# First block's end: order of logits and weight low parts, of pooling and short convolution, of the output units' parts, and layer norm's PSUM banks

## The chip, the cores and the metric

One core of a Trainium2 chip runs the whole program. The metric is the device time of one execution in microseconds (us), as the median of several runs.

## The reference

Two blocks run one after the other on 512 tokens of width 1024. The change concerns the first block alone:

```python
h = rms_norm(x, norm1_g); z = h @ w_in                    # 1024 -> 9 x 256
y_pool  = pool_mixer(z_pool, pool_w, pool_scale)          # running means over 2, 4, 8, 16 tokens, then 64x64 matrices
y_sconv = s_b * causal_dwconv(s_c * s_h, sconv_w)         # 3 taps
u = c_a * sigmoid(c_g); u = causal_dwconv(u, conf_dw_w) + conf_dw_b     # 31 taps
y_conf  = silu(layer_norm(u, conf_ln_g, conf_ln_b))
y_attn  = diff_attention(q, k, v, ...)                    # 4 heads, two softmaxes each, bias by distance
x = x + concat([y_pool, y_sconv, y_conf, y_attn]) @ w_out
x = x + (silu(h2 @ w_gate) * (h2 @ w_up)) @ w_down        # h2 = rms_norm(x, norm2_g)
```

The second block prepends 16 meta tokens and has two layers of its own.

## The kernel before, in words

Activations lie with features on the partitions and tokens along the row. Every large product is made of three matmuls of 128x128 by 128x512 in a reduced-precision float format: a value is split into a high part (a cast, ScalarE) and a low part (value minus high part, VectorE), and high x high, high x low and low x high are summed in PSUM. `f_acc` (L171, matmuls at L179) does this for one output tile of 128 features: 8 input tiles give 24 matmuls. After each group of three it calls `tick`, which emits the next piece of a background generator, here attention.

Weights come by `weights` (L145): SP loads 512 KB into one of two buffers `wraw`, ScalarE casts it in two halves to `whi` (L164), VectorE makes the two low parts `wlo` (L165), each with four buffers, so that two sets of weights are present. A load waits until the low parts of the set two before it are made; a cast waits until TensorE has used the tile it overwrites.

The order on each engine is set by a scheduler at build time. It takes instructions by priority as their inputs become ready in its own model of time. `first()` gives a raised priority (weights, evacuations), `chain()` a far higher one (offset 100000), and `behind(ins, name)` an order edge between two instructions of one engine. On the chip each engine then works its list strictly in order.

`layer1` (L493) is the first block's mixer. In order of the program: the gates of the long convolution (ca, cg), values, keys and queries; attention starts as a background pipeline (`pipe` with the stages `logits`, `wait`, `turn`, `values`, `wait`, `finish`, 16 items, one step per three ticks). `logits` makes two score tiles in the PSUM banks "a" (L656), reduces each on VectorE with the bias added (L658), exponentiates on ScalarE (L660), and combines the two softmaxes (L665 to L667). `turn` transposes them in banks "b" (L209), `values` multiplies by v (L686). The long convolution of 31 taps is 60 instructions on VectorE (L725) with ordinary priority, so they fill its gaps; its result is y. Then four projections by `fproj` (two output tiles each): z for pooling, two for the short convolution (sc, evacuated by L740), and sb (evacuated by L552). After these stand the pooling chain (L745 to L759), the short convolution (L760 to L766), `mix` of its two rows, the pool matrices (L770, L772) and `mix` of their two rows. `mix` splits a result into a high part (cast, L117) and a low part (L118) in one of the four `mx` buffers, which the gates and the short convolution's temporaries use in turn as well. Then layer norm of y: sums over features by matmul (L779, L787, L248) in the PSUM banks "b", the last product at L798.

The output projection is made in two halves by `add_out` (L332): first pooling and short convolution (`mixed[:4]`, L799), then attention and conformer rows (`mixed[4:]`), each in four units of two output tiles; each tile takes its four rows in order, 12 matmuls, and is added to x (L356). `add_out` has an argument `late=n` that makes the first unit take the first n rows for both its tiles before the others; these calls don't use it. `finish(att)` between the halves emits what is left of attention.

At the start, `setup` (L375) loads x in tiles and the first two sets of weights by the queues of SP and ScalarE in an order written by hand. `layer1` splits x (L257 and L258) and these weights (L511 and L512), and the first 48 matmuls (L579) follow tile by tile. `tables` (L458) builds the tables of the position bias on GpSimd: it loads relb and the meta tokens by GpSimd's own DMA queue (L469, L470), copies runs of buckets (L482), writes the tables to DRAM (L484) and later reads the bias tile B from there (L490).

Of the kernel before, what the change touches and what calls it, by code (L numbers as in the profile page):

```python
# [18 lines left out]
S = 512  # L19
# [46 lines left out]
class Kern:  # L66
# [78 lines left out]
    def weights(self, nk, ncol):  # L145

        if self.ahead:
            return self.ahead.pop(0)
        src = self.io["w"]
        n = nk * ncol  # L150
        out = [], []
        with self.first():
            raw = self.wp.tile([128, 1024], F32, name="wraw", bufs=2)
            self.queue(self.nc.sync, raw[:, :n], bass.AP(tensor=src.tensor, offset=src.offset + self.wi, ap=[[n, 128], [1, n]]))
            step = 512 // ncol
            for k0 in range(0, nk, step):
                k1 = min(k0 + step, nk)
                c = slice(k0 * ncol, k1 * ncol)
                w = c.stop - c.start
                if self.keep:  # L160
                    hi, lo = (self.row(n) for n in ("hhi", "hlo"))
                else:
                    hi, lo = (self.wp.tile([128, 512], F32R, name=n, bufs=4) for n in ("whi", "wlo"))
                self.nc.scalar.copy(hi[:, :w], raw[:, c])  # L164
                self.lo.tensor_tensor(out=lo[:, :w], in0=raw[:, c], in1=hi[:, :w].bitcast(F32), op=OP.subtract)  # L165
                for t, o in zip((hi, lo), out):
                    o += [t[:, k * ncol:(k + 1) * ncol] for k in range(k1 - k0)]
            self.wi += 128 * n
        return out
# [205 lines left out]
    def setup(self):  # L375
# [9 lines left out]
        with self.first():  # L385
# [13 lines left out]
            w(nc.scalar, 1, 0, 512)  # L399
            w(nc.sync, 0, 256, 512)  # L400
            x(nc.scalar, 1, 2)
# [56 lines left out]
    def tables(self):  # L458
# [4 lines left out]
        with self.tc.tile_pool(name="setup", bufs=1) as p:  # L463

            rb = p.tile([128, 3, 32], F32, name="relb")
            for h in range(4):
                src = self.io["relb"]
                src = bass.AP(tensor=src.tensor, offset=src.offset + 32 * h, ap=[[0, COPIES], [128, 3], [1, 32]])
                nc.gpsimd.dma_start(rb[h * COPIES:(h + 1) * COPIES], src)  # L469
            nc.gpsimd.dma_start(self.xs[:, :, 0:M], io["meta"].rearrange("k p t -> p k t"))  # L470
# [22 lines left out]
    def layer1(self):  # L493
# [44 lines left out]
        with tc.tile_pool(name="l1", bufs=1, reuse_waits="tile") as p:  # L538
# [4 lines left out]
            def fproj(out, evac=None):  # L543
                for f in range(2):
                    w = self.weights(8, 128)
                    ps = self.mm()
# [100 lines left out]
            def logits(i, h):  # L647
# [5 lines left out]
                for m in range(2):  # L653
# [3 lines left out]
                    with self.chain():  # L657
                        nc.vector.tensor_tensor_reduce(out=e, in0=ps[:, :W], in1=B1[:, h, 384 - 128 * i:],  # L658
                                                       scale=-1.0, scalar=BIG, op0=OP.add, op1=OP.min, accum_out=st[:, m:m + 1])
# [4 lines left out]
                with self.chain():  # L664
                    nc.vector.reciprocal(r, st[:, 2:4])  # L665
                    nc.vector.tensor_scalar(r[:, 1:2], r[:, 1:2], st[:, 2:3], lam[:, 0:1], op0=OP.mult, op1=OP.mult)
# [74 lines left out]
            fproj(sb)  # L741
            mixed = [None] * 8
            with self.chain():
# [16 lines left out]
                nc.vector.tensor_tensor(out=sc[:, :, PADS:], in0=sc[:, :, PADS:], in1=rb2[:, None, :].to_broadcast([128, 2, S]), op=OP.mult)  # L760
                sw = self.cols[:, COLS["sconv"][0]:COLS["sconv"][0] + 6].rearrange("p (f k) -> p f k", f=2)
                for f in range(2):
                    nc.scalar.mul(sh[:, f], sc[:, f, 0:S], sw[:, f, 0:1])
                    for k in (1, 2):
                        nc.vector.scalar_tensor_tensor(sh[:, f], sc[:, f, k:k + S], sw[:, f, k:k + 1], sh[:, f], op0=OP.mult, op1=OP.add)
                    nc.vector.tensor_tensor(out=sb[:, f], in0=sb[:, f], in1=sh[:, f], op=OP.mult)  # L766
                    mixed[2 + f] = self.mix(sb[:, f], M, T)
# [6 lines left out]

            ones = self.m1
            with self.chain():
                ps = self.ch("b")
# [6 lines left out]
                ps = self.ch("b")  # L784
# [5 lines left out]
                ps = self.ch("b")  # L790
# [8 lines left out]
            self.add_out(mixed[:4], X)  # L799
# [11 lines left out]
            self.add_out(mixed[4:], X, after)  # L811
# [999 lines left out]
```

## Time and profile before

| | |
|---|---|
| median of 3 runs | 1182.95 us (1182.59 to 1184.75) |
| profiled execution | 1182.28 us |
| its span | 1180.5 us |
| TensorE busy | 1157.7 us, 98% |
| VectorE busy | 792.2 us, 67% |
| ScalarE busy | 627.4 us, 53% |
| GpSimd busy | 66.9 us, 6% |
| instructions | 18912 |

The span runs from the first to the last instruction of the profile; the run's time holds a little more around it. TensorE's share is high over the whole span, so the rows below look at stretches of it: the first 30 us and the first block's end, from 100 to 180 us. A bracket behind an instruction gives the idle time of its engine before it, and what ended it. An instruction counts as busy from its modelled start to its end; matmuls overlap, so that a record may be longer than the pace at which they follow each other.

### The profile page before, as it was taken

What the parts mean: (1) busy time and instruction counts of PE and PEld (TensorE: products, weight loads), DVE (VectorE), ACT (ScalarE), POOL (GpSimd) and SP (SyncE); (2) the same over time, 40 slices, a digit from 0 to 9 for tenths busy, and PEclk for the clock granted to TensorE, in tenths of its full rate; (3) what the DMA queues carried; (4) which work ended last, traced back from release to release, by engine and by line L of the source; (5) the groups of instructions that cost most, each with busy time, mean ns of one, the idle gap of its engine ahead of it and who ended that gap; (6) DMA issues with size and microseconds to landing.
All of it is one profiled execution on the core that took longest, in us unless ns stands there. A gap on an engine that the chain in (4) does not pass through costs nothing.

```text
span 1180.5 us, 18912 instructions
## 1 busy us (share of the span) xinstructions
PE 1157.7 (98%) x7094; PEld 994.4 (84%) x7094; DVE 792.2 (67%) x1765; ACT 627.4 (53%) x1404; POOL 66.9 (6%) x175
## 2 busy tenths in 40 slices
PE   8999799999999999999999999999999999999997
PEld 6988588888888888888899899899999888887786
DVE  7999957544433444445799999666567476776782
ACT  6578646433322333344546346667555488777533
POOL 8000002000000000002000000000011000000000
PEclk9999999999999999999999999999999999999999
DMA  7421112332233233223322112222223221421221
GB/s 245 123 83 54 52 56 90 98 99 91 84 99 114 97 95 102 78 95 126 104 72 72 55 54 72 74 72 75 71 66 127 79 72 55 108 61 53 85 72 72
DMA packets 32908, 101.83 MB, mean 86 GB/s; under 512 B 4128, under 2 KB 4960, under 8 KB 32816
## 3 DMA queue, kind: packets, MB, share of 16 engines
q1 hardware_dynamic: 30784, 96.48, 26.3%
q0 software_dynamic: 880, 2.25, 0.7%
q10 hardware_dynamic: 1152, 1.89, 0.5%
q8 instruction: 56, 0.92, 0.3%
q14 instruction: 36, 0.29, 0.1%
HBM read 96.42 MB, written 3.10 MB: 84 GB/s over the span
## 4 chain that ended last, share of the span: by engine, by line
PE 87%; DVE 8%; ACT 2%; DMA 1%; issue 1%; POOL 0%; DVEq 0%; ACTq 0%; POOLq 0%; SPq 0%
PE mm L179 70%; PE psb L209 3%; DVE wlo L165 2%; DVE y L725 2%; PE pso L1187 1%; PE pso L1443 1%; PE psa L1580 1%; PE mm L1580 1%; PE psa L1428 1%; DVE sc L1041 1%; PE pso L686 1%; PE psb L1428 1%; DVE m L1040 1%; DMA x<-in_x 1%; PE psa L1149 1%
## 5 line engine op out<-in xcount | busy, mean ns | idle before, releaser
L179 PE MATMUL mm<-hhi,whi 128*128 128x512 f32 (+2 forms) x1280 | 432.4, 338 | 0.0
L179 PE MATMUL mm<-hhi,wlo 128*128 128x512 f32 (+2 forms) x1280 | 426.0, 333 | 2.9 <-DVE wlo L165 2.9
L179 PE MATMUL mm<-hlo,whi 128*128 128x512 f32 (+2 forms) x1280 | 425.1, 332 | 0.0
L164 ACT CAST whi<-wraw 128x512 fp32r<-128x512 f32 x346 | 205.2, 594 | 277.9 <-PE mm L179 251.4
L165 DVE TENSOR_TENSOR wlo<-wraw,whi 128x512 fp32r<-128x512 f32 x346 | 231.1, 671 | 137.6 <-ACT whi L164 118.0
L179 PEld LDWEIGHTS mm<-hhi,wlo 128*128 128x128 f32 x1280 | 241.5, 189 | 25.3 <-DVE wlo L165 3.0
L179 PEld LDWEIGHTS mm<-hhi,whi 128*128 128x128 f32 x1280 | 241.9, 189 | 23.0 <-issue 1.4
L179 PEld LDWEIGHTS mm<-hlo,whi 128*128 128x128 f32 x1280 | 241.5, 189 | 20.9 <-issue 0.2
L179 PE MATMUL mm<-mx,whi 128*128 128x512 f32 (+2 forms) x384 | 92.5, 333 | 5.8 <-ACT mx L117 5.6
L179 PEld LDWEIGHTS mm<-mx,whi 128*128 128x128 f32 x384 | 64.8, 192 | 12.9 <-ACT mx L117 6.3
L830 DVE TENSOR_TENSOR gu<-mm,rb 128x512 f32<-128x512 f32 x44 | 30.4, 691 | 66.8 <-PE mm L179 66.8
L271 POOL TENSOR_TENSOR acc<-acc,sq 128x528 f32<-128x528 f32 (+1 forms) x18 | 25.6, 1423 | 771.8 <-ACT sq L269 771.8
L179 PE MATMUL mm<-hidh,whi 128*128 128x512 f32 x176 | 68.5, 389 | 0.0
L179 PE MATMUL mm<-hidh,wlo 128*128 128x512 f32 x176 | 68.5, 389 | 0.0
L179 PE MATMUL mm<-hidl,whi 128*128 128x512 f32 x176 | 68.5, 389 | 0.0
L179 PE MATMUL mm<-mx,wlo 128*128 128x512 f32 (+2 forms) x192 | 61.9, 324 | 0.0
L725 DVE SCALAR_TENSOR_TENSOR y<-u,cols,y 128x512 f32<-128x512 f32 x60 | 42.3, 742 | 0.1
L370 DVE TENSOR_TENSOR tmp<-mm,rb 128x272 f32<-128x272 f32 (+2 forms) x60 | 28.8, 479 | 17.6 <-PE mm L179 17.0
L356 DVE TENSOR_TENSOR x<-x,mm 128x512 f32<-128x512 f32 (+2 forms) x56 | 29.8, 535 | 15.0 <-PE mm L179 14.7
L179 PEld LDWEIGHTS mm<-mx,wlo 128*128 128x128 f32 x192 | 36.6, 191 | 2.7 <-issue 0.2
L179 PEld LDWEIGHTS mm<-hidh,whi 128*128 128x128 f32 x176 | 33.0, 188 | 6.9
L179 PEld LDWEIGHTS mm<-hidl,whi 128*128 128x128 f32 x176 | 33.0, 188 | 6.8
(444 smaller groups left out, 1820.9 us busy)
## 6 DMA issues: line engine op xcount, KB each, us to landing
wraw<-in_w SPq DMA_DIRECT2D x144, 512.0 KB, 3.5
wraw<-in_w SPq DMA_DIRECT2D x16, 384.0 KB, 3.0
wraw<-in_w SPq DMA_DIRECT2D x16, 320.0 KB, 2.8
bh<-tab SPq DMA_DIRECT2D x16, 132.0 KB, 3.6
mx<-cqk SPq DMA_DIRECT2D x8, 132.0 KB, 4.9
x<-in_x SPq DMA_DIRECT2D x4, 256.0 KB, 5.0
B<-tab POOLq DMA_DIRECT2D x4, 256.0 KB, 8.7
out<-L ACTq DMA_DIRECT2D x4, 256.0 KB, 2.4
```

The costliest lines, as they stand in the source:

```text
L164: self.nc.scalar.copy(hi[:, :w], raw[:, c])
L165: self.lo.tensor_tensor(out=lo[:, :w], in0=raw[:, c], in1=hi[:, :w].bitcast(F32), op=OP.subtract)
L179: nc.tensor.matmul(ps[b], lhsT=ww[i][:, f0:f0 + nf], rhs=aa[:, t0:t1], start=first and i == 0 and j == 0, stop=last and i == n - 1 and j == 2)
L209: self.nc.tensor.transpose(out, in_, self.ident[:n, :n])
L271: e.tensor_tensor(out=acc[:, c0:c1], in0=acc[:, c0:c1], in1=sq[:, c0:c1], op=OP.add)
L356: nc.vector.tensor_tensor(out=x, in0=x, in1=p, op=OP.add)
L370: self.nc.vector.tensor_tensor(out=out[:, t0:t1], in0=p, in1=rb[:nf, t0:t1], op=OP.mult)
L686: nc.tensor.matmul(o[:, h * 64:h * 64 + 64], lhsT=pT[:, j * 128:(j + 1) * 128], rhs=vt[:, j, h * 64:h * 64 + 64], start=j == 0, stop=j == i)
L725: nc.vector.scalar_tensor_tensor(y[:, f], u[:, f, k:k + S], cw[:, f, k:k + 1], y[:, f], op0=OP.mult, op1=OP.add)
L830: nc.vector.tensor_tensor(out=t[:, g], in0=ps, in1=rbx, op=OP.mult)
L1428: nc.tensor.matmul(z, lhsT=self.trir[:n, :n], rhs=part, start=False, stop=True, skip_group_check=True)
L1580: nc.tensor.matmul(ps[half], lhsT=aa[:, k], rhs=ww[:, :512], start=False, stop=k == 3 and j == 2, skip_group_check=True)
```

## The change

It has six parts.

1. `weights` remembers the name of the last low part that it issued (`self.last`), and each logits reduction (L658) gets an order edge behind it.
2. The projection sb moves behind pooling and the pool matrices. Its evacuation is now `short`, which multiplies by the norm's factor and, for the first tile, does the whole short convolution; each tile's `mix` follows. With `then=(4, 256)` the first set of the output projection's weights is loaded before the second tile's matmuls.
3. Layer norm's three PSUM tiles come from the banks "a" (of the logits), not "b".
4. Both halves of the output projection take `late=2`: their first unit takes the first two rows (pooling, attention) for both tiles first.
5. The small step at L666 is a scalar_tensor_tensor instead of a tensor_scalar.
6. At the start, the second set's first weight load is halved with the second x tile between the halves, and relb and the meta tokens are loaded by SP's queue instead of GpSimd's.

```diff
--- before.py
+++ after.py
@@ -162,7 +162,7 @@
                 self.nc.scalar.copy(hi[:, :w], raw[:, c])
-                self.lo.tensor_tensor(out=lo[:, :w], in0=raw[:, c], in1=hi[:, :w].bitcast(F32), op=OP.subtract)
+                self.last = self.lo.tensor_tensor(out=lo[:, :w], in0=raw[:, c], in1=hi[:, :w].bitcast(F32), op=OP.subtract).ins.name
                 for t, o in zip((hi, lo), out):
@@ -396,9 +396,10 @@
             w(nc.sync, 0, 0, 256)
-            w(nc.scalar, 1, 0, 512)
+            w(nc.scalar, 1, 0, 256)
+            x(nc.scalar, 1, 2)
             w(nc.sync, 0, 256, 512)
-            x(nc.scalar, 1, 2)
+            w(nc.scalar, 1, 256, 512)
             x(nc.sync, 2, 3)
@@ -466,8 +467,8 @@
                 src = bass.AP(tensor=src.tensor, offset=src.offset + 32 * h, ap=[[0, COPIES], [128, 3], [1, 32]])
-                nc.gpsimd.dma_start(rb[h * COPIES:(h + 1) * COPIES], src)
-            nc.gpsimd.dma_start(self.xs[:, :, 0:M], io["meta"].rearrange("k p t -> p k t"))
+                nc.sync.dma_start(rb[h * COPIES:(h + 1) * COPIES], src)
+            nc.sync.dma_start(self.xs[:, :, 0:M], io["meta"].rearrange("k p t -> p k t"))
@@ -540,9 +541,11 @@
-            def fproj(out, evac=None):
+            def fproj(out, evac=None, then=None):
                 for f in range(2):
                     w = self.weights(8, 128)
+                    if f == 1 and then:
+                        self.ahead.append(self.weights(*then))
                     ps = self.mm()
@@ -655,15 +658,17 @@
                     with self.chain():
-                        nc.vector.tensor_tensor_reduce(out=e, in0=ps[:, :W], in1=B1[:, h, 384 - 128 * i:],
-                                                       scale=-1.0, scalar=BIG, op0=OP.add, op1=OP.min, accum_out=st[:, m:m + 1])
+                        ins = nc.vector.tensor_tensor_reduce(out=e, in0=ps[:, :W], in1=B1[:, h, 384 - 128 * i:],
+                                                             scale=-1.0, scalar=BIG, op0=OP.add, op1=OP.min, accum_out=st[:, m:m + 1])
...
+                        self.behind(ins.ins, self.last)
                         nc.scalar.activation(e, e, AF.Exp, scale=-1.0, bias=st[:, m:m + 1], accum_out=st[:, 2 + m:3 + m])
...
                     nc.vector.reciprocal(r, st[:, 2:4])
-                    nc.vector.tensor_scalar(r[:, 1:2], r[:, 1:2], st[:, 2:3], lam[:, 0:1], op0=OP.mult, op1=OP.mult)
+                    nc.vector.scalar_tensor_tensor(r[:, 1:2], r[:, 1:2], st[:, 2:3], lam[:, 0:1], op0=OP.mult, op1=OP.mult)
                     nc.vector.scalar_tensor_tensor(es[0], es[1], r[:, 1:2], es[0], op0=OP.mult, op1=OP.add)
@@ -738,7 +743,6 @@
             fproj(None, evac=lambda f, ps: nc.vector.tensor_tensor(out=sc[:, f, PADS:], in0=ps, in1=sc[:, f, PADS:], op=OP.mult))
-            fproj(sb)
             mixed = [None] * 8
@@ -757,14 +761,6 @@
                     nc.vector.tensor_tensor(out=z[:, f, PADP:], in0=a[:, PADP:], in1=z[:, f, PADP:], op=OP.subtract)
-                nc.vector.tensor_tensor(out=sc[:, :, PADS:], in0=sc[:, :, PADS:], in1=rb2[:, None, :].to_broadcast([128, 2, S]), op=OP.mult)
-                sw = self.cols[:, COLS["sconv"][0]:COLS["sconv"][0] + 6].rearrange("p (f k) -> p f k", f=2)
-                for f in range(2):
-                    nc.scalar.mul(sh[:, f], sc[:, f, 0:S], sw[:, f, 0:1])
-                    for k in (1, 2):
-                        nc.vector.scalar_tensor_tensor(sh[:, f], sc[:, f, k:k + S], sw[:, f, k:k + 1], sh[:, f], op0=OP.mult, op1=OP.add)
-                    nc.vector.tensor_tensor(out=sb[:, f], in0=sb[:, f], in1=sh[:, f], op=OP.mult)
-                    mixed[2 + f] = self.mix(sb[:, f], M, T)
             for f in range(2):
@@ -772,22 +768,38 @@
+            def short(f, ps):
...
+                nc.vector.tensor_tensor(out=sb[:, f], in0=ps, in1=rbx, op=OP.mult)
+                with self.chain():
+                    if f == 0:
+                        nc.vector.tensor_tensor(out=sc[:, :, PADS:], in0=sc[:, :, PADS:], in1=rb2[:, None, :].to_broadcast([128, 2, S]), op=OP.mult)
+                        sw = self.cols[:, COLS["sconv"][0]:COLS["sconv"][0] + 6].rearrange("p (f k) -> p f k", f=2)
+                        for i in range(2):
+                            nc.scalar.mul(sh[:, i], sc[:, i, 0:S], sw[:, i, 0:1])
+                            for k in (1, 2):
+                                nc.vector.scalar_tensor_tensor(sh[:, i], sc[:, i, k:k + S], sw[:, i, k:k + 1], sh[:, i], op0=OP.mult, op1=OP.add)
+                    nc.vector.tensor_tensor(out=sb[:, f], in0=sb[:, f], in1=sh[:, f], op=OP.mult)
+                    mixed[2 + f] = self.mix(sb[:, f], M, T)
...
+            fproj(None, evac=short, then=(4, 256))
...
             ones = self.m1
             with self.chain():
-                ps = self.ch("b")
+                ps = self.ch("a")
                 for f in range(2):
...
                     nc.scalar.square(ysq[:, f], y[:, f])
-                ps = self.ch("b")
+                ps = self.ch("a")
                 for t in range(4):
...
                 self.rstd(yr, ps[:, :4], 256, True)
-                ps = self.ch("b")
+                ps = self.ch("a")
                 for t in range(4):
@@ -796,7 +808,7 @@
                     nc.vector.tensor_tensor(out=y[:, f], in0=y[:, f], in1=ysq[:, f], op=OP.mult)
-            self.add_out(mixed[:4], X)
+            self.add_out(mixed[:4], X, late=2)
             self.finish(att)
@@ -808,7 +820,7 @@
-            self.add_out(mixed[4:], X, after)
+            self.add_out(mixed[4:], X, after, late=2)
         return act2, acc
...
     def ffn(self, act, acc):
```

## Rows read from the trace of the kernel before

**Rows 1.** Page, part 1: busy time of TensorE (PE) and of its weight loads (PEld) and the other engines, share of the span, instructions.

```profile
PE 1157.7 (98%) x7094; PEld 994.4 (84%) x7094; DVE 792.2 (67%) x1765; ACT 627.4 (53%) x1404; POOL 66.9 (6%) x175
```

**Rows 2.** Waits of TensorE from 60 to 180 us: who waited, for whom; us in total, times, longest us.

```profile
PE mm L179 <- ACT mx L117: 5.3, 1, 5.3
PE mm L179 <- DVE wlo L165: 2.9, 1, 2.9
```

**Rows 3.** Chain that ended last, in order of time: start us, us, engine, tile and line, number of instructions. The first piece opens the first output unit of the first half of the output projection; the second is the long stretch of the feed-forward part.

```profile
146.82 5.07 PE mm L179 x12
...
204.46 358.84 PE mm L179 x1583
```

**Rows 4.** Windows of TensorE: length, PE busy us (instructions), granted clock as a share of full speed, DMA share, GB/s.

```profile
141.40:146.80 5.40, 0.13 (x1) 0.78 0.41 145
146.80:151.70 4.90, 4.88 (x12) 0.54 0.19 75
```

**Rows 5.** TensorE in order of time: start us, us, line, operation, out<-in, count, and in brackets the idle time before it and what ended it. The first is in the last short-convolution projection, the second the first layer-norm sum over the second half of y.

```profile
138.96 0.50 PE L179 MATMUL mm<-hhi,wlo 128*128 128x512 f32 x1 [2.86 <-DVE wlo L165]
...
151.72 1.02 PE L779 MATMUL psb<-y,m 128*128 128x512 f32 x2
```

**Rows 6.** VectorE (DVE) in order of time, same columns: low parts of weights (L165), evacuations of the short-convolution projection (L552) and their products (L766), low parts of the mixed rows (L118), the long convolution (L725), the last product of the conformer branch (L798).

```profile
113.51 0.69 DVE L165 TENSOR_TENSOR wlo<-wraw,whi 128x512 fp32r<-128x512 f32 x1
...
136.19 0.67 DVE L552 TENSOR_TENSOR sb<-mm,rb 128x512 f32<-128x512 f32 x1
...
138.22 0.68 DVE L165 TENSOR_TENSOR wlo<-wraw,whi 128x512 fp32r<-128x512 f32 x1
...
143.71 0.68 DVE L552 TENSOR_TENSOR sb<-mm,rb 128x512 f32<-128x512 f32 x1
...
144.91 0.69 DVE L766 TENSOR_TENSOR sb<-sb,mx 128x512 f32<-128x512 f32 x1
...
146.89 1.29 DVE L118 TENSOR_TENSOR mx<-z,mx 128x512 fp32r<-128x512 f32 x2
148.09 1.53 DVE L725 SCALAR_TENSOR_TENSOR y<-u,cols,y 128x512 f32<-128x512 f32 x2
...
167.99 0.68 DVE L798 TENSOR_TENSOR y<-y,ysq 128x512 f32<-128x512 f32 x1
```

**Rows 7.** ScalarE (ACT) in order of time, same columns: casts of weights (L164) and of mixed rows (L117).

```profile
115.82 0.62 ACT L164 CAST whi<-wraw 128x512 fp32r<-128x512 f32 x1
...
124.96 0.61 ACT L164 CAST whi<-wraw 128x512 fp32r<-128x512 f32 x1
...
145.63 0.62 ACT L117 CAST mx<-sb 128x512 fp32r<-128x512 f32 x1 [2.04 <-DVE sb L766]
146.15 1.13 ACT L117 CAST mx<-z 128x512 fp32r<-128x512 f32 x2
...
175.62 0.62 ACT L117 CAST mx<-yT 128x512 fp32r<-128x512 f32 x1 [3.09 <-PE mm L179]
...
177.19 1.14 ACT L117 CAST mx<-y 128x512 fp32r<-128x512 f32 x2
```

**Rows 8.** Window of all engines, from 105.3 to 138.2 us: length, busy us (instructions) of PE, PEld, DVE, ACT and POOL, granted clock, DMA share, GB/s.

```profile
105.30:138.20 32.90, 30.81 (x175) 25.55 (x173) 30.40 (x94) 25.28 (x71) 0.00 (x0) 1.00 0.06 20
```

**Rows 9.** Groups of VectorE's instructions in the same window: shapes and count, busy us, mean ns of one, idle us before them and releaser.

```profile
L765 DVE SCALAR_TENSOR_TENSOR mx<-mx,cols 128x512 f32<-128x512 f32 x4 | 3.0, 745 | 0.0
L666 DVE TENSOR_SCALAR rd<-rd,st,rowp 128x1 f32<-128x1 f32 x10 | 2.7, 268 | 0.0
L725 DVE SCALAR_TENSOR_TENSOR y<-u,cols,y 128x512 f32<-128x512 f32 x3 | 2.2, 732 | 0.0
...
L665 DVE RECIPROCAL rd<-st 128x2 f32<-128x2 f32 x10 | 1.6, 158 | 0.5 <-ACT e L660 0.5
...
L760 DVE TENSOR_TENSOR mx<-mx,rb 128x1024 f32<-128x1024 f32 x1 | 1.2, 1216 | 0.0
```

**Rows 10.** GpSimd (POOL) in order of time: the copies that build the first bias table, and the issue of the loads of the bias tile B.

```profile
8.57 5.35 POOL L482 COPY t<-relb 128x399 f32<-128x399 f32 x14 [3.75 <-DMA relb<-in_relb]
...
26.65 2.21 POOL L490 DMA_DIRECT2D B<-tab  x4
```

**Rows 11.** Instructions of line L658, the reduction of a logits tile: count, ns min/median/max, first and last start us, shapes.

```profile
L658 DVE CUSTOM_DVE_ANT_0 e<-psa,B x32: 276/481/693, 86.1 to 133.5; 128x128 f32<-128x128 f32 x8, 128x256 f32<-128x256 f32 x8, 128x384 f32<-128x384 f32 x8, 128x512 f32<-128x512 f32 x8
```

**Rows 12.** Page, part 6: loads of B: count, KB each, median us from issue to landing.

```profile
B<-tab POOLq DMA_DIRECT2D x4, 256.0 KB, 8.7
```

**Rows 13.** Waits of the SP queue (its DMA issues) from 0 to 190 us.

```profile
SPq L140 <- DVE wlo L165: 132.3, 20, 27.7
```

**Rows 14.** The start, all engines in order of time: row 6.09 is the first pair of weight low parts, 7.15 the second x tile's high part, 8.57 the second pair of weight low parts, 10.43 the fourth x tile's high part, 13.07 the low parts of x tiles 5 to 8, 14.52 the first matmul that waited for them.

```profile
6.09 0.76 DVE L512 TENSOR_TENSOR wlo<-mx,whi 128x256 fp32r<-128x256 f32 x2 [0.33 <-ACT whi L511]
...
7.15 0.72 ACT L257 ACTIVATE hhi<-x,cols 128x512 fp32r<-128x512 f32 x1 [0.78 <-DMA x<-in_x]
...
8.57 1.07 DVE L512 TENSOR_TENSOR wlo<-mx,whi 128x256 fp32r<-128x256 f32 x2
...
10.43 0.72 ACT L257 ACTIVATE hhi<-x,cols 128x512 fp32r<-128x512 f32 x1 [1.33 <-DMA x<-in_x]
...
13.07 3.38 DVE L258 SCALAR_TENSOR_TENSOR hlo<-x,cols,hhi 128x512 fp32r<-128x512 f32 x4
...
14.52 0.49 PE L579 MATMUL psa<-hlo,whi 128*128 128x512 f32 x1 [0.86 <-DVE hlo L258]
```

## Prediction

> **What bounds the kernel now.** I read the page first: TensorE is busy 1157.7 us, 98% of the span [rows 1], so all that any change of order can win is the 22.8 us in which it is not, and what it loses at a lower clock. Then the waits of TensorE from 60 to 180 us: only two count, 2.9 us for a low part of weights and 5.3 us for the cast of a mixed row [rows 2]. Both lie at the first block's end. The chain in order of time shows a third loss there: the 12 matmuls behind the second wait take 5.07 us, 0.42 us each, where the 1583 matmuls of the long feed-forward stretch take 358.84 us, 0.227 us each [rows 3]. The granted clock is 0.54 in that stretch, near the lower of its two levels (1.2 GHz; the upper is 2.4), and TensorE had been idle before it [rows 4]. At 0.227 us the 12 would take 2.72 us, so 2.35 us are lost. Together 2.86 + 5.29 + 2.35 = **10.5 us** hang on this one place.
>
> Why it waits: VectorE. From 105.3 to 138.2 us it is busy 30.40 of 32.90 us [rows 8], nearly all of it the attention chain, which has priority over the weights' low parts. The cast at 115.82 gave the high part, its low part came at 138.22; the previous one came at 113.51, so for 24.7 us there was none [rows 6, 7]. TensorE stood for exactly this one at 138.96 [rows 5]. The second wait is a chain: the last projection is evacuated at 143.71, multiplied at 144.91, cast at 145.63 [rows 6, 7]. TensorE's first matmul there takes a pooling row, but that row's cast stands behind on ScalarE, at 146.15, its low part at 146.89 [rows 6, 7].
>
> **The change part by part.** The sum is made against the profiled execution, 1182.28 us (span 1180.5); the median of the runs is 1182.95, 0.67 higher, and I add that at the end.
>
> *Logits behind low parts.* Every logits reduction follows the last weight low part issued before it. This removes the 2.86 us wait. What is queued behind the waiting reduction is the rest of VectorE's attention chain, and TensorE's next logits, which have two PSUM banks. A set's buffers come free two projections earlier (the cast at 115.82 is for the set used from about 126), so ordinarily the low part is ready long before and the edge costs nothing but order. Only the set loaded ahead (`then`) is tight: its cast stands at 124.96, as the projection before ends [rows 7]; then 0.62 us of cast and 0.68 us of low part stand ahead of one logits step. Between 0 and 1.3 us; I take 0.3, since VectorE has other chain work meanwhile.
>
> *Pooling first, short convolution later.* The two pool matmuls (same cost, other place), casts and low parts come before the last projection and their mx buffers are those of the gates, free since long. The output unit starts with 12 pooling matmuls, 12 x 0.227 = 2.72 us, which cover the last evacuation (0.68), product (0.69), cast and low part: 143.71 to the end of the cast at 146.25 is 2.54 us [rows 3, 6, 7]. So the 5.29 us and the slow clock go if VectorE keeps up. It must do in that window, beside what it does now: three low parts (2.0 us) and the two pooling low parts (1.29 us) [rows 6]; the short convolution (1.2 + 3.0 us) [rows 9] changes place but stays. The step L666 becomes a scalar_tensor_tensor: bounded by its old 268 ns (no gain) and by the 158 ns of the small reciprocal [rows 9]; nearest in shape is the latter, so 10 x 0.11 = 1.1 us less. The 2.2 us of long convolution (y) can slip out of it [rows 9]. 30.40 + 2.0 + 1.3 - 1.1 - 2.2 = 30.4 us of work beside 30.81 us on TensorE [rows 8]: even. VectorE's idle 2.5 us of now may return as a wait on TensorE: 0 to 2.5 us, I take 0.8.
>
> *Layer norm in the logits' banks; second half.* The y that slips is done later. Now y ends at 149.62 and the conformer row at 168.67 [rows 6], 19.05 us of chain. VectorE's total work is unchanged, so I leave y's end there. The banks let attention's last transposes go without queueing behind layer norm's sums; its end is then early and no limit. The first half of the output projection runs from 146.82 to about 175.6, when the first attention row can be cast [rows 3, 7]: 28.8 us, less 2.35 of slow clock. If it starts near 139, TensorE is at the second half at 165.4 and, with attention's 12 matmuls first, needs the conformer rows at 168.2, plus their cast and low part from 168.67: about 2 us late. The chain should lose the 2.1 us until its first sum at 151.72 [rows 5, 6], which stood behind slow matmuls. Between 0 and 3.5 us; I take 1.0.
>
> *The start.* The first load of weights on ScalarE's queue is halved and the second x tile goes between; relb and meta leave GpSimd's queue for SP's, five issues. ScalarE waits 0.78 us for the second x tile and 1.33 us for the fourth [rows 14]; the first gets earlier, the fourth has the same bytes ahead of it. TensorE waits 0.86 us at 14.52 for a low part of a group whose four take 3.38 us [rows 14]. Between 1.5 us gained and 0.5 lost (one more issue ahead of later tiles); I take 0.5 gained. On SP the issues fall into its wait for weight buffers and cost nothing. The copies on GpSimd move some 8 us later, and B with them; the cover is wide (second rival).
> As to those copies, the pair of low parts at 8.57, beside them, took 1.07 us where the pair at 6.09 took 0.76 [rows 10, 14]. The Trainium skill (GPSIMD Engine Reference, 1. Specifications) says that GpSimd's way to SBUF is shared with VectorE and contends with instructions that read two SBUF inputs; by that the start would win its full 1.5 us, and the sum would be 1 us lower. I stay with 0.5, since the copies may take from VectorE later what they leave it here.
>
> Sum: 1182.28 - 10.5 + 0.3 + 0.8 + 1.0 - 0.5 = 1173.4; with 0.67 for the median, **1174.0 us**.
>
> **The rivals.**
> *A (forecast), 0.58:* as above, 1171 to 1177.
> *B, 0.22: the conformer branch becomes the bound.* With TensorE 10 us earlier, y is still filler on a full VectorE, and layer norm's sums stand in TensorE's fixed order. If y slips by the 3 us and the chain keeps its 19 us, TensorE waits 5 us for the conformer rows instead of 1: 1178. For it: VectorE 92% busy [rows 8]. Against: it still stood idle for 2.5 us there.
> *C, 0.11: it does not do what it says.* The scheduler keeps y and the short convolution in front of the last evacuation. Low parts come early, but the same VectorE work ends at 148.2 less its 2.5 us of idle time: the second wait and the slow clock stay in large part, and what the first wait gave goes into waiting for logits: about 1181.
> *D, 0.09, slower: the bias table comes too late.* relb's issue is now in SP's queue, which stands 132.3 us in 20 waits for weight low parts [rows 13]. From the copies' start at 8.57 to B's issue at 26.65 and landing 8.7 us later, 28.9 us with the issuing (2.21), to the first logits at 86.1 [rows 10 to 12], there are some 48 us to spare. If relb stood behind enough weight loads to land after 57 us, the logits, and TensorE in its fixed order, wait us for us; at 70 us that is 13 us against 10 gained: 1186. Against: 132 of SP's 190 us are such waits, so that issues which wait for nothing find free places early.
>
> **How the numbers follow.** The time is A's. The range: below, all new waits at nought and the start at 1.5: 1170.9, so 1170.5; above, B and A's bounds, to 1180.0. C and D, 0.20, are left out. A change under 0.2% (2.4 us) can't be told from none. Faster by that: A, B and little of C, 0.82; same: most of C, 0.10; slower: D, 0.08.
>
> **What would show it.** Right: no wait of TensorE over 1 us between 100 and 165 us, the clock at 1.00 throughout, low parts evenly spaced between the logits, the first mixed-row matmul near 139 us, the feed-forward part starting some 9 us earlier. B: a wait for the cast of y or for layer norm, near 165. C: the waits of the before still there at other sizes. D: first logits after 87 us. Wrong at the root, if TensorE has no idle time there and the span has not fallen by it.

## The result, and the profile after

The changed kernel takes 1176.34 us (median of 4 runs, 1175.28 to 1177.78) against 1183.07 before: a ratio of 0.9941, interval 0.9929 to 0.9953, 6.7 us less. The forecast was 1174.0 in a range of 1170.5 to 1180.0. The profiled execution of after is the longest of its four, 1177.78 us (span 1176.0).

Page, part 1, of after, to be set against [rows 1]: busy time, share of the span and instructions of each engine.

```profile
PE 1159.9 (99%) x7094; PEld 996.0 (85%) x7094; DVE 791.5 (67%) x1765; ACT 625.6 (53%) x1404; POOL 57.4 (5%) x170
```

TensorE's idle time has gone from 22.8 to 16.1 us with the same 7094 matmuls, while its busy time is 2.2 us longer, so that the span of this execution is 4.5 us shorter. Where the idle time went is read from TensorE's waits in after, 60 to 180 us, against [rows 2]:

```profile
PE mm L179 <- ACT mx L117: 2.2, 1, 2.2
PE mm L179 <- DVE mx L118: 0.2, 1, 0.2
```

The 2.9 and the 5.3 us are gone; what stands here is another wait, later and for another row. The windows of after show the place (length, busy us and instructions of PE, PEld, DVE, ACT and POOL, granted clock, DMA share, GB/s), against [rows 4, 8]:

```profile
100.00:120.00 20.00, 20.00 (x108) 16.63 (x107) 19.69 (x68) 15.66 (x51) 0.00 (x0) 1.00 0.25 80
120.00:140.00 20.00, 20.00 (x116) 16.58 (x114) 17.74 (x47) 14.32 (x36) 0.00 (x0) 1.00 0.16 53
140.00:160.00 20.00, 20.00 (x101) 15.91 (x100) 17.84 (x37) 8.01 (x20) 0.00 (x0) 1.00 0.24 79
160.00:172.00 12.00, 9.83 (x53) 7.58 (x51) 7.37 (x16) 9.07 (x24) 0.00 (x0) 1.00 0.14 44
172.00:177.00 5.00, 4.83 (x15) 3.75 (x15) 3.60 (x7) 2.57 (x5) 0.00 (x0) 0.66 0.15 35
```

From 100 to 160 us TensorE never stops and the clock stays at 1.00. Then come 2.17 us of wait and, behind it, 15 matmuls in 4.83 us at a mean clock of 0.66; at the 0.227 us of [rows 3] they would take 3.4, so 1.4 us are lost there. The chain of after in order of time (start us, us, what) names the new wait's cause, and answers to [rows 3]:

```profile
163.18 1.70 PE mm L179 x7
164.88 0.47 PE psa L248 x4
165.35 0.23 PE mm L179
165.58 0.23 PE psb L209 x2
165.81 0.02 issue
165.84 0.48 ACT yT L715
166.31 1.41 ACT y L808 x2
167.72 1.04 ACT ysq L218 x2
168.76 1.04 ACT ysq L219 x2
169.80 0.53 ACT ysq L220
170.33 0.02 issue
170.35 1.29 DVE y L810 x2
171.65 0.61 DVE mx L118
172.26 0.04 issue
172.30 27.06 PE mm L179 x111
...
200.57 4.58 PE mm L179 x20
```

The last attention row is ready at 166.3 (yT, L715), but its cast stands on ScalarE behind four us of the conformer branch's activations and starts at 170.74. The feed-forward stretch starts at 200.57 instead of 204.46, 3.9 us earlier.

### The profile page after: what moved, and what is told of

Same layout as the page of the kernel before. It is cut to its first block, busy times and chain, and to the rows that moved or that the text cites. A ratio compares the mean times of both kernels' runs of the same rounds, so it can differ in the third digit from the quotient of the medians.

```text
span 1176.0 us, 18907 instructions
## 1 busy us (share of the span) xinstructions
PE 1159.9 (99%) x7094; PEld 996.0 (85%) x7094; DVE 791.5 (67%) x1765; ACT 625.6 (53%) x1404; POOL 57.4 (5%) x170
## 4 chain that ended last, share of the span: by engine, by line
PE 87%; DVE 8%; ACT 2%; DMA 1%; issue 1%; SPq 0%; POOL 0%; DVEq 0%; ACTq 0%; POOLq 0%
PE mm L179 70%; PE psb L209 3%; DVE y L730 2%; DVE wlo L165 2%; PE pso L1199 1%; PE pso L1455 1%; PE psa L1592 1%; PE mm L1592 1%; PE pso L691 1%; PE psa L1440 1%; DVE sc L1053 1%; DMA wraw<-in_w 1%; PE psb L1440 1%; DVE m L1052 1%; PE psa L1161 1%
## 5 line engine op out<-in xcount | busy, mean ns | idle before, releaser
L164 ACT CAST whi<-wraw 128x512 fp32r<-128x512 f32 x346 | 205.1, 594 | 285.6 <-PE mm L179 262.5
L165 DVE TENSOR_TENSOR wlo<-wraw,whi 128x512 fp32r<-128x512 f32 x346 | 231.1, 671 | 139.9 <-ACT whi L164 119.7
L370 DVE TENSOR_TENSOR tmp<-mm,rb 128x272 f32<-128x272 f32 (+2 forms) x60 | 28.8, 480 | 17.6 <-PE mm L179 17.1
L356 DVE TENSOR_TENSOR x<-x,mm 128x512 f32<-128x512 f32 (+2 forms) x56 | 29.8, 535 | 14.0 <-PE mm L179 13.4
L179 PEld LDWEIGHTS mm<-hidh,wlo 128*128 128x128 f32 x176 | 33.0, 188 | 6.8
```

The costliest lines, as they stand in the source:

```text
L165: self.last = self.lo.tensor_tensor(out=lo[:, :w], in0=raw[:, c], in1=hi[:, :w].bitcast(F32), op=OP.subtract).ins.name
L179: nc.tensor.matmul(ps[b], lhsT=ww[i][:, f0:f0 + nf], rhs=aa[:, t0:t1], start=first and i == 0 and j == 0, stop=last and i == n - 1 and j == 2)
L356: nc.vector.tensor_tensor(out=x, in0=x, in1=p, op=OP.add)
L370: self.nc.vector.tensor_tensor(out=out[:, t0:t1], in0=p, in1=rb[:nf, t0:t1], op=OP.mult)
```

## The experiments

Three parts of the change are looked at apart: the **edge** (logits behind low parts), the **move** (last projection behind the pooling rows, short convolution in its evacuation, with the small parts: the start, the set split ahead, pairs of rows first, L671) and the **banks** (layer norm's PSUM tiles). With before and after, the twelve runs cover all eight combinations. The kernel before had medians of 1183.59 to 1183.94 us beside them.

| parts | run | median us | ratio, interval |
|---|---|---|---|
| edge | e5 | 1179.38 | 0.9965 (0.9952 to 0.9979) |
| move | e7 | 1180.40 | 0.9970 (0.9960 to 0.9981) |
| banks | e11 | 1178.91 | 0.9960 (0.9946 to 0.9973) |
| edge, move | e9 | 1181.73 | 0.9985 (0.9977 to 0.9994) |
| edge, banks | e10 | 1174.95 | 0.9927 (0.9915 to 0.9939) |
| move, banks | e3 | 1174.02 | 0.9920 (0.9907 to 0.9934) |
| move without small parts, banks | e12 | 1174.81 | 0.9926 (0.9913 to 0.9940) |
| all three | after | 1176.34 | 0.9941 (0.9929 to 0.9953) |

**e1, the start as before.** The changed kernel with the load order and the table loads of the kernel before:

```diff
-            w(nc.scalar, 1, 0, 256)
+            w(nc.scalar, 1, 0, 512)
+            w(nc.sync, 0, 256, 512)
             x(nc.scalar, 1, 2)
-            w(nc.sync, 0, 256, 512)
-            w(nc.scalar, 1, 256, 512)
...
-                nc.sync.dma_start(rb[h * COPIES:(h + 1) * COPIES], src)
-            nc.sync.dma_start(self.xs[:, :, 0:M], io["meta"].rearrange("k p t -> p k t"))
+                nc.gpsimd.dma_start(rb[h * COPIES:(h + 1) * COPIES], src)
+            nc.gpsimd.dma_start(self.xs[:, :, 0:M], io["meta"].rearrange("k p t -> p k t"))
```

> The changed kernel with the start as it was (weights of the second set in one load of 256 KB ahead of the second x tile, relb and meta by GpSimd's queue). Theory: in the trace of the changed kernel the start's matmuls end 0.7 us earlier, but the norm's sums of squares end 0.5 us later, TensorE waits 1.04 us for them at 24 us and then runs at 0.55 of its clock until 30 us, so that the start costs 2.1 us at the first L730; undone, the long convolution starts near 35.0 us instead of 37.2 and the time falls by 1 to 2 us. Rival: the slow clock there is chance of that one execution (its span is 1 to 2.5 us longer than those of the three others); then the time stays within 0.7 us.

Measured 1177.04 us (1175.55 to 1177.22), ratio 0.9941 (0.9929 to 0.9954), the same as after: the rival holds. The start edits bring nothing that can be told from none.

**e2, only the table loads back on GpSimd's queue** (the second half of that diff).

> The changed kernel with only relb and meta back on GpSimd's queue; the halved weight load and earlier second x tile stay. If the late table copies beside the sums of squares (one addition there took 1.00 us instead of 0.68) are what costs, the wait at 24 us goes back to 0.3 us, the clock stays at 1.00 and the start keeps its 0.7 us: 1 to 2.7 us faster than the changed kernel. If the halved load is what costs, the time is as the changed kernel's and e1 alone is faster.

Measured 1176.08 us (1174.42 to 1176.98), ratio 0.9934 (0.9922 to 0.9947): no difference from after either.

**e3, without the edge.**

```diff
-                        self.behind(ins.ins, self.last)
```

> The changed kernel without the order edge of the logits behind the weights' low parts. Theory: the low parts are starved again between about 118 and 138 us, TensorE waits 2 to 4 us for one of them: 2 to 5 us slower than the changed kernel. Rival: moving the short convolution and pooling rows already frees VectorE enough: within 0.7 us.

Measured 1174.02 us (1173.16 to 1175.34): 2.3 us faster than with it. The theory that the edge is needed fell. Here are VectorE's low parts, its last logits reduction (L661) and the end of its long convolution in e3, in order of time (start us, us, line, operation, out<-in, count):

```profile
116.92 0.68 DVE L165 TENSOR_TENSOR wlo<-wraw,whi 128x512 fp32r<-128x512 f32 x1
...
136.43 0.68 DVE L661 CUSTOM_DVE_ANT_0 e<-psa,B 128x512 f32<-128x512 f32 x1
...
141.43 2.49 DVE L165 TENSOR_TENSOR wlo<-wraw,whi 128x512 fp32r<-128x512 f32 x4
...
153.28 0.75 DVE L729 SCALAR_TENSOR_TENSOR y<-u,cols,y 128x512 f32<-128x512 f32 x1
```

No low part runs for 24.5 us, as before the change, and yet TensorE waits for none. Its waits from 60 to 210 us:

```profile
PE psb L209 <- DVE ot L702: 1.0, 1, 1.0
PE mm L179 <- DVE mx L118: 0.2, 1, 0.2
```

In e2, which has the edge, the last logits reduction runs later and the long convolution ends later:

```profile
138.76 0.69 DVE L661 CUSTOM_DVE_ANT_0 e<-psa,B 128x512 f32<-128x512 f32 x1 [0.27 <-PE psa L659]
...
154.28 1.53 DVE L730 SCALAR_TENSOR_TENSOR y<-u,cols,y 128x512 f32<-128x512 f32 x2
```

The last reduction comes 2.3 us later, and y ends at 155.8 instead of 154.0. Layer norm follows it, and the attention row's cast follows layer norm on ScalarE: the wait of 2.2 us is there in after, e1 and e2, and not in e3.

**e4, layer norm's block behind attention's end in program order**, edge kept (`add_out(mixed[:4])`, `finish(att)` and the mix of yT moved ahead of the block `ones = self.m1`).

> The changed kernel with the layer norm block placed, in the program, behind the first half of the output projection and the attention rows' split, so that attention's last steps and the cast of its rows stand ahead of layer norm's activations on ScalarE. Theory: the 2.2 us wait at 171.4 us is ScalarE's order (the attention rows' cast stood behind eight activations of the conformer branch, and attention's last root behind layer norm's); it goes, and with it some 2 us of slow clock: 3 to 4 us faster than the changed kernel, about 1172.5. Rival: the conformer rows themselves are late (y ended at 157.8 instead of 149.6); then the wait only moves behind attention's 12 matmuls, to the cast of y, and at most 1 us is won.

Measured 1177.27 us (1175.81 to 1177.87), ratio 0.9946. The wait for the cast went, as meant, and one of 2.99 us at the feed-forward part's norm (195.92) took its place: the time was not won, it was passed on. Neither the theory's 3 to 4 us nor the rival's wait for y came.

**e5, the kernel before with the edge alone.**

```diff
+                        self.behind(ins.ins, self.last)
```

> The kernel before, with one edit of the change alone: every logits reduction follows the low part of weights issued before it. Theory of the prediction (the edge wins the 2.86 us wait): no wait for a low part at 139, the projections end 2.9 us earlier, the wait for the pooling row stays near 5.3 us; 1183.6 - 2.5 = about 1181, at best 1180.7. Theory after the run without the edge (the order of VectorE's work only changes places, the sum of its work decides): the wait for a low part is gone, but the cast of the mixed row comes no earlier, so the second wait grows from 5.3 to about 8 us; 1183 to 1184, no change.

Measured 1179.38 us, 4.6 less, more than either theory gave: the 2.9 us wait went and the other shrank from 5.3 to 4.0 instead of growing. So the edge does win on the kernel before; it is the company of the move that makes it a loss.

**e6, e3 with the rows in plain order** (both `late=2` taken out).

> The changed kernel without the edge, and with both halves of the first block's output projection in the plain order again (no pair of mixed rows is taken first through a whole output unit). Theory (the pooling rows first are the cover for the last projection's evacuation, product, cast and low part): TensorE has 6 instead of 12 pooling matmuls, 1.4 us, before the short convolution's rows are due 2.5 us after the projection's end: a wait of about 1.2 us and matmuls at the low clock behind it, some 1 to 2 us; in the second half the same with attention's rows ahead of the conformer's: 6 x 0.227 = 1.4 us later need is lost, a wait of 0 to 2 us. 1174.0 + 1.5 to 4 = 1175.5 to 1178. Rival (the order of the rows is worth nothing, because pooling rows come first in either order and VectorE has room): no wait over 0.5 us at either half, 1174 +- 0.7.

Measured 1173.76 us (1172.72 to 1174.74): the pairs of rows taken first are worth nothing, the rival's time holds. TensorE's one wait is the 1.0 us of e3, for attention's end, over the 0.5 that the rival allowed.

**e7, e3 with layer norm's tiles in attention's banks.**

```diff
-                ps = self.ch("a")
+                ps = self.ch("b")
```

> The changed kernel without the edge, with layer norm's three PSUM tiles taken from the banks of attention's transposes and values, as before the change. Theory (the banks matter little where attention is not the last to end): attention's roots and layer norm's sums queue for two banks in turn, some 1 to 2 us of delay for one of them, hidden; 1174.0 to 1175. Rival (the banks set when attention ends): a wait for the cast of attention's row or of a conformer row of 2 us or more near 165 us, as in the changed kernel, 1176 to 1177.

Measured 1180.40 us (1179.76 to 1180.78): taking attention's banks for these three tiles costs 6.4 us, far over the theory and the rival's worst. Layer norm's matmuls (L790, L798, L248, one line for each of its three tiles) and attention's last transposes (L209) on those banks in e7, 140 to 176 us (count, ns min/median/max, first and last start us):

```profile
L790 PE MATMUL psb<-y,m x2: 590/590/591, 155.2 to 155.6; 128*128 128x512 f32 x2
L798 PE MATMUL psb<-ones,ysq x16: 164/250/271, 157.9 to 160.1; 128*128 128x1 f32 x16
L248 PE MATMUL psb<-keep,yr x4: 272/273/323, 161.8 to 162.2; 128*128 128x128 f32 x4
L209 PE MATMUL psb<-keep,e x8: 272/273/329, 163.3 to 164.3; 128*128 128x128 f32 x8
```

Attention's transposes in e3:

```profile
L209 PE MATMUL psb<-keep,e x8: 272/272/328, 140.6 to 141.8; 128*128 128x128 f32 x8
```

Attention's last eight transposes start at 163.3 instead of 140.6, behind layer norm's third tile. In the program, too, they stand behind those tiles: by the source, 48 ticks of attention come before layer norm, and `turn` of its last two items, eight transposes, is emitted only during the output projection. Layer norm's first tile has its first sums at 137.4 and its last at 155.6, since they need the end of the long convolution; its second and third tile then take the two banks in turn. TensorE then waits at attention's end, 4.3 us of it for one product:

```profile
PE psb L209 <- DVE ot L702: 4.3, 1, 4.3
PE mm L179 <- ACT mx L117: 1.2, 1, 1.2
```

**e8, e3 without the set split ahead** (`then=(4, 256)` taken out).

> The changed kernel without the edge, and without the set of weights that is split ahead of the last projection (the output projection's first set is split after it, as before the change). Theory: its high part and low part are ready late: in the profile without the edge no low part ran between 117 and 141.4 us, and the first mixed-row matmul at 134.6 uses the high parts first. If the output projection's set is split only when the last projection is issued, its casts stand behind ScalarE's chain work: a wait at 135 of 0.5 to 2 us with slow clock behind it, 1174.5 to 1177. Rival (the scheduler brings the split forward by itself, since its buffers are free long before): no wait, 1174 +- 0.7.

Measured 1173.98 us (1173.62 to 1177.42): nothing lost in the median, the rival holds. The set split ahead, at which the prediction called the edge tight, isn't needed. The five runs lie wide apart; the profiled one is the longest (1177.42) and has from 60 to 210 us the waits of e3 and one of 0.2 us. What it has besides are two stretches at a mean clock under 1.00, from 25 to 30 us (0.66) and from 650 to 660 us (0.83), neither of which the trace of e3 has.

**e9, the changed kernel with layer norm in attention's banks**, the edit of e7 with the edge kept.

> The changed kernel, edge included, with layer norm's three PSUM tiles in attention's two banks, as before the change. Without the edge this cost 6.4 us, since attention's last transposes stood behind the three layer norm tiles (163.3 instead of 140.6 us). Theory (the banks tie attention's end to layer norm's; the edge only moves both): the same wait for the last attention row near 165 to 172 us, 1176.3 + 4 to 6.5 = 1180 to 1183. Rival (the edge brings attention's last logits so late that its transposes come behind layer norm's sums in any case, so that the banks are worth little with the edge): 1176 to 1178.

Measured 1181.73 us (1181.12 to 1183.42), inside the theory's 1180 to 1183. Its windows, same columns as above:

```profile
100.00:150.00 50.00, 50.00 (x266) 41.12 (x266) 46.83 (x131) 33.77 (x95) 0.00 (x0) 1.00 0.21 65
150.00:180.00 30.00, 23.50 (x111) 18.15 (x110) 17.99 (x32) 15.48 (x33) 0.00 (x0) 0.83 0.22 68
```

These two rows are the plainest of the study. Edge and move do all that was forecast of them: from 100 to 150 us TensorE never stops, where before it stood for 8.2 us. From 150 to 180, where before had no idle time, 6.5 us of it return, and the clock falls there.

**e10, the kernel before with edge and banks.**

> The kernel before with two edits: the edge and layer norm's tiles in the logits' banks; pooling, short convolution, the order of the rows and the start as before. Theory (the move of the last projection behind the pooling rows is a part of its own): the 4.0 us wait for the pooling row's cast at 143 us stays, what lies behind layer norm gains little, since with a late start of the first half nothing at its end was waited for: 1178.5 to 1179.5, as the edge alone. Rival (the banks free attention's end, VectorE then has its last chain work before the evacuation): the wait shrinks to 0 to 2 us, 1175 to 1177.

Measured 1174.95 us (1173.78 to 1175.94): the rival holds. Without any move the 4.0 us wait of e5 is gone; no wait of TensorE is over 0.7 us.

**e11, the kernel before with the banks alone.**

> The kernel before with layer norm's three tiles in the logits' banks and nothing else. Theory (the banks are worth something only once the first half of the output projection starts early enough to reach its attention rows before they are there): both waits as before, 2.9 and 5.3 us, 1183 to 1184. Rival (the banks are a gain by themselves): 1178 to 1181.

Measured 1178.91 us (1177.27 to 1179.43): the rival holds, the banks gain 5 us by themselves. The rows that say why are TensorE's from 135 to 146 us in e11 (in brackets the idle time before and what ended it):

```profile
135.18 1.00 PE L686 MATMUL pso<-vtok,pT 128*128 128x64 f32 x8
136.66 0.41 PE L209 MATMUL psb<-keep,ot 128*128 128x128 f32 x2 [0.48 <-DVE rd L665]
136.91 0.60 PE L209 MATMUL psb<-keep,e 128*128 128x128 f32 x4
138.19 1.10 PE L686 MATMUL pso<-vtok,pT 128*128 128x64 f32 x8 [0.67 <-ACT pT L676]
139.13 0.61 PE L209 MATMUL psb<-keep,e 128*128 128x128 f32 x4
139.49 0.48 PE L179 MATMUL mm<-hhi,wlo 128*128 128x512 f32 x1
...
141.88 1.00 PE L686 MATMUL pso<-vtok,pT 128*128 128x64 f32 x8
145.16 1.46 PE L179 MATMUL mm<-mx,whi 128*128 128x512 f32 x4 [2.28 <-ACT mx L117]
```

VectorE's low part for the matmul at 139.49, in e11:

```profile
138.54 0.68 DVE L165 TENSOR_TENSOR wlo<-wraw,whi 128x512 fp32r<-128x512 f32 x1
```

It comes no earlier than the 138.22 of [rows 6]. But TensorE no longer stands 2.86 us for it: it does attention's last transposes and value products in that time. The three waits left in these rows come to 3.4 us, where before had 8.2. In the kernel before, those transposes ran here:

```profile
L209 PE MATMUL psb<-keep,e x8: 272/272/327, 160.7 to 161.8; 128*128 128x128 f32 x8
```

**e12, move and banks without any small part.** The kernel before with the projection moved and the three `ch("a")`.

> The kernel before with two edits of the change and no other: the last projection moved behind the pooling rows, its evacuation followed by the short convolution, and layer norm's three PSUM tiles in the logits' banks. The edge, the set split ahead, the pair of rows taken first, the product of the lambda step, and the start are as before. Theory (these two are the whole gain; the banks let attention's last transposes run before layer norm's sums, and the move takes the short convolution's product from in front of the output projection): no wait over 1.2 us from 100 to 180 us, 1173.5 to 1174.7, a ratio of 0.9915 to 0.993. Rival (the small parts, each under 0.3 us alone, add up): 1175 to 1177.

Measured 1174.81 us (1173.95 to 1175.27), 0.1 us over the theory's span of times and inside its ratios. Two edits carry at least the whole gain: their median is 1.5 us under that of the whole change, though the intervals of the two ratios overlap.

## Why the prediction was right, and where it was not

**The 10.5 us at one place: right in size.** In after both waits and the slow clock of [rows 2 to 4] are gone, and the first matmul on a mixed row is at 136.87 against a forecast of 139. Two of the signs that were named for being right did not come: the feed-forward part starts 3.9 us earlier and not 9, and the low parts are not evenly spaced (none starts between 119.5 and 133.7), though TensorE waits for none of them.

**What brings them: wrong.** The working gave 2.86 us to the edge and 7.64 to the move, and the banks nothing ("its end is then early and no limit"). By the table the banks are the one part that gains in any company: 5.0 us alone, 4.4 beside the edge, 6.4 beside the move, 5.4 beside both. Edge and move replace each other. Alone they gain 4.6 and 3.5, with the banks 4.0 and 4.9; together without the banks only 2.1. Added to the other, each costs 1.3 to 2.4 us by the medians; in each such pair the two intervals overlap, so these four sizes are uncertain. The view that was missing is the use of attention's banks by line: two banks are given out in turn, layer norm's three tiles stand there ahead of attention's last ones, and so eight transposes ran some 23 us later (160.7 in the kernel before, from 136.9 in e11). They cost twice. In the kernel before, TensorE stood idle with this work held back (8.2 us of waits against 3.4 in e11); and once the first waits are cured, attention's end becomes the bound (e7, e9). That the order of the banks is the cause is read from the source, from these rows and from four pairs of kernels that differ in it alone; a third bank for attention was not tried.

**The edge, +0.3: mis-sized.** "Costs nothing but order" was wrong: with the move and the banks it costs 2.3 us (e3 against after; the four kernels without it have medians of 1173.8 to 1174.8, the three with it 1176.1 to 1177.0). It makes logits wait for low parts that nobody waits for yet. The forecast had named the way ("What is queued behind the waiting reduction") and not priced it.

**VectorE too full, +0.8:** no wait of TensorE for VectorE before the output projection; 0. The step L671 takes 212 ns instead of 267, a saving of 0.055 us a step where 0.11 was taken.

**Conformer rows late, +1.0 (0 to 3.5):** the place was right, the row was not. TensorE waits for the attention row's cast, behind the conformer's activations on ScalarE: 2.17 + 0.17 us, and 1.4 of slow clock, 3.7 in all, just over the bound. The terms behind the forecast were each further off, and that their errors partly cancelled was luck. y was left at 149.62 and ended at 157.84; its chain was put at 19.05 less up to 2.1 us and took 13.8; the conformer rows came at 171.65. TensorE was due at the second half at 165.4 and finished the first at 169.23: the first half took 32.4 us from its first matmul, while the forecast read 28.8 off the cast at 175.62 of the kernel before, whose second half in fact begins at 177.40. Rival B (1178, a wait near 165) described the outcome nearly, with y slipping further than its 3 us and the chain not keeping its 19; the wait in after is half of B's size. ScalarE's order at this place is the term that was not worked out.

**The start, -0.5:** e1 shows 0.7 us, not to be told from none. In the profiled execution of after the start even lost some 2 us (first logits reduction at 88.2 against 86.1 in [rows 11]), by a wait and a slow clock that the same start in e4 does not have.

**The sum with what was measured:** 1182.28 - 10.5 + 3.7 = 1175.5, plus 0.67 is 1176.2, against 1176.34. For the profiled execution alone, with the 2.1 us that it lost at the start, it is 1177.6 against 1177.78. The forecast came near because the size of the loss in [rows 2 to 4] capped what any cure could give, not because the parts were priced rightly; the banks, without which the same change takes 1181.73 us (e9), had no price in it.

**Rivals C and D** fell: the waits are gone, and the first logits reduction stands at 88.2 us, with no wait of TensorE for the bias table.

## What to carry to other kernels

Before pricing a wait as "VectorE is late", look at what else TensorE could have done in it, and which buffer holds that work back; here two PSUM banks given out in turn held ready work for over 20 us without one of TensorE's waits being put down to them. Two cures of one wait need not add up (4.6 and 3.5 us alone, 2.1 together): try each alone and in pairs. When a wait goes, look for where the idle time returns further on, as it did in e4 and e9.

## What the runs showed of the hardware

VectorE's low parts, which read two operands in SBUF, slow down beside GpSimd's additions. From e4, VectorE and then GpSimd in order of time:

```profile
183.49 1.52 DVE L165 TENSOR_TENSOR wlo<-wraw,whi 128x512 fp32r<-128x512 f32 x1
...
185.59 1.77 DVE L165 TENSOR_TENSOR wlo<-wraw,whi 128x512 fp32r<-128x512 f32 x1
...
187.89 0.68 DVE L165 TENSOR_TENSOR wlo<-wraw,whi 128x512 fp32r<-128x512 f32 x1
...
189.43 0.68 DVE L356 TENSOR_TENSOR x<-x,mm 128x512 f32<-128x512 f32 x1
```

```profile
183.16 1.30 POOL L271 TENSOR_TENSOR acc<-acc,sq 128x512 f32<-128x512 f32 x1 [0.74 <-ACT sq L269]
185.45 1.38 POOL L271 TENSOR_TENSOR acc<-acc,sq 128x512 f32<-128x512 f32 x1 [0.98 <-ACT sq L269]
189.32 1.34 POOL L271 TENSOR_TENSOR acc<-acc,sq 128x512 f32<-128x512 f32 x1 [2.50 <-ACT sq L269]
```

The same subtraction takes 1.52 and 1.77 us while GpSimd adds, and 0.68 when it doesn't. The addition to x (L356), which reads one operand in PSUM, keeps its 0.68 us in the middle of a GpSimd addition. The rule that the prediction weighed is that GpSimd's SBUF interfaces are shared with VectorE, with contention for VectorE instructions that have two SBUF inputs (the Trainium skill, GPSIMD Engine Reference, 1. Specifications); these rows agree with it. Beside GpSimd's copies of the bias table the picture is mixed: of the pair in [rows 14], both beside copies, one took 0.42 and one 0.74 us, and the 128x512 low parts of L165 that ran beside the copies took 0.67 to 0.73 us in all traces, hardly more than alone. At the start it is worth little: in after the second pair takes 0.42 and 0.43 us without the copies beside it, yet e1 shows no gain in the time.

In some executions an early wait is followed by a slow clock. In the profiled execution of after TensorE waits 1.04 us at 24.0, and the window behind it is slow. In that of e4, with the same start, no wait there is over 0.5 us, and the window is not slow. First after, then e4:

```profile
25.00:30.00 5.00, 5.00 (x18) 3.82 (x18) 3.46 (x17) 2.45 (x7) 4.69 (x20) 0.66 0.27 106
```

```profile
25.00:30.00 5.00, 4.51 (x22) 3.47 (x21) 3.61 (x14) 3.67 (x8) 4.69 (x20) 1.00 0.47 129
```

In the first 18 matmuls run in 5 us of busy time, in the second 22 in 4.51. Of the other traces only that of e8 has such a wait (1.11 us at 24.0) and such a window (0.66); in the rest no wait between 20 and 30 us is over 0.63 us, and the clock stays at 1.00. Why the same start waits longer in some executions stays open.
